# Both heads of a pair in one product: the scans of a hybrid mixer with block-diagonal queries and states

## The chip, the cores and the metric

The kernel runs on one core of a Trainium2 chip. TensorE (PE in the profile; its weight loads PEld) multiplies, VectorE (DVE), ScalarE (ACT) and GpSimd (POOL) do the rest of the arithmetic, and SyncE (SP) issues the DMAs. The metric is the device time of one launch in microseconds; the comparison is between the kernel before and the kernel with the change.

## The reference

A trunk of two layers over 1024 tokens of width 1024. The first layer's mixer splits one projection between four mLSTM heads and four retention heads, each with keys and queries of 64 and values of 128; the second is a Mamba-2 mixer; each is followed by an MLP. Only the first mixer changes. Both of its groups run over chunks of 128 tokens with a carried state. For retention (mLSTM has gates in place of the constant decay, and a normaliser that is carried as one more column of the state):

```python
s = jnp.einsum('bcthk,bcshk->bctsh', q, k) * decay
intra = jnp.einsum('bctsh,bcshv->bcthv', s, v)
d_r = jnp.einsum('lh,bclhk,bclhv->bchkv', w_k, k, v)
def step(r, dr):
    return chunk_decay[:, None, None] * r + dr, r
_, r_prev = lax.scan(step, jnp.zeros((bsz, nh, dk, dv), F32), jnp.moveaxis(d_r, 1, 0))
inter = w_q[None, None, :, :, None] * jnp.einsum('bcthk,bchkv->bcthv', q, r_prev)
return (intra + inter).reshape(bsz, seq, nh, dv)
```

## The kernel before

The residual stream lies in SBUF for the whole kernel. Large products are made of three products of high and low parts (`proj_in` at L136, `proj_nat` at L152, `proj_out` at L180). A tile framework derives the waits and, when the program is built, an order for each engine's queue: instructions that are ready are taken by their place in the program, so later work moves into gaps of earlier work, and the queues then run in that fixed order.

`hybrid` goes through the eight heads in four pairs, in the order 2, 3 (retention), 0, 1 (mLSTM). For a pair it projects values into `va` (tokens on partitions), then q and k into `qT` and `kT`, with head j of the pair on partitions 64j to 64j+63, tokens along the free dimension. Then comes the scan over eight chunks, then two gate projections (`hgate`), the head norm, and the output projection. Each scan's chunk does the following, all in fp32:

- L490 transposes k of both heads into PSUM (`tr`), L497 scales it by token into `kw`.
- L508, per head: scores, `kT` by `qT` on that head's 64 partitions, into the head's own PSUM tile `bank[j]`.
- L515 and L521 (mLSTM) or L523 (retention), per head: the scores under the decay mask, into `pt`.
- L528: queries scaled for the carried state, `qs`.
- L536 and L540, per head: `pt` by values, then `qs` by the carried state on 64 partitions, added up in the same PSUM tile; L543 copies the sum to `num`.
- L548, per head: `kw` by values into 64 of the 128 partitions of `dc`; L553 or L555 makes the new state from the old one and `dc`, both heads in one instruction, since the state of head j lies on partitions 64j to 64j+63.

The scan of a pair takes four PSUM tiles a chunk from a pool of five (`sc`). `headnorm` (L687 to L709) takes statistics of `num` on VectorE and two powers a half on GpSimd (L702, L706 for their kinds of pair). The weights' split into high and low parts is on ScalarE (L93) and VectorE (L94). The small tile `hnwr` (L402 to L406) holds the head norms' weights until they are transposed, early in the kernel. In the second mixer, L829, L838, L843 and L858 are the transposes and products of its scan, L832 a scaling of a transposed tile.

## Time and profile before

| | us |
|---|---|
| time, median of 3 runs | 2815.06 (2813.73 to 2817.12) |
| time of the profiled execution | 2813.8 |
| its span, first to last instruction | 2812.0 |
| TensorE busy | 2735.5 (97%) |
| VectorE busy | 1696.3 (60%) |
| ScalarE busy | 933.9 (33%) |
| GpSimd busy | 500.3 (18%) |

Busy time of TensorE counts from the start of a matmul to a modelled end, and neighbours overlap; the distance between two starts is what a product costs the queue. The granted clock of TensorE is full but for a few short stretches (mean 0.993). A product of fp32 operands appears as two records, each of a weight load (PEld) and a matmul. In a row, 64*128 after the tile names means a stationary operand of 64 rows and 128 columns.

### The profile page before, as it was taken

How to read it: one execution, taken by the hardware profiler on the slowest of the kernel's cores; microseconds unless marked ns; L12 is line 12 of the kernel's file. 1: busy time of each engine (PE TensorE's matmuls, PEld its weight loads, DVE VectorE, ACT ScalarE, POOL GpSimd, SP SyncE). 2: the span in 40 equal slices, each digit the busy share in tenths (PEclk: the TensorE clock that was granted, in tenths of full speed). 3: DMA queues.
4: the chain of work that ended last, by engine and by line, in shares of the span. 5: the costliest groups of instructions: out<-in, count | busy, mean ns of one | idle time of the engine just before them, and what ended most of it. 6: DMA issues, size and time to landing. Idle time of an engine off the chain costs nothing.

```text
span 2812.0 us, 33165 instructions
## 1 busy us (share of the span) xinstructions
PE 2735.5 (97%) x13149; PEld 2206.2 (78%) x13149; DVE 1696.3 (60%) x2794; ACT 933.9 (33%) x1547; POOL 500.3 (18%) x454
## 2 busy tenths in 40 slices
PE   8999999999999999899999999999999999999997
PEld 7788787888888888687787777777778888888885
DVE  5544436645656445876667667666676566654457
ACT  5131223322222222443433434344344222222223
POOL 1000000322233222300000000000013222322223
PEclk9999999999999999899999999999999999999999
DMA  4021210211111111032212222122221111110111
GB/s 157 23 77 31 60 53 23 68 45 60 60 60 46 37 39 55 23 81 74 67 54 70 67 67 75 51 70 68 59 62 53 60 60 60 53 42 27 60 38 60
DMA packets 199050, 161.47 MB, mean 57 GB/s; under 512 B 8952, under 2 KB 177840, under 8 KB 198768
## 3 DMA queue, kind: packets, MB, share of 16 engines
q1 hardware_dynamic: 198896, 159.36, 19.3%
q8 instruction: 103, 1.69, 0.2%
q14 instruction: 51, 0.42, 0.0%
HBM read 154.68 MB, written 4.62 MB: 57 GB/s over the span
## 4 chain that ended last, share of the span: by engine, by line
PE 91%; DMA 4%; ACT 2%; DVE 2%; POOL 1%; issue 0%; SPq 0%; DVEq 0%; ACTq 0%; POOLq 0%
PE mmin L136 49%; PE mmout L260 21%; PE mmout L180 9%; DMA cb<-cs_d 4%; PE mmnat L152 3%; PE yp L838 1%; PE pt L223 1%; PE bank L536 1%; PE bank L540 1%; ACT cb L816 1%; POOL h L355 1%; DVE un L206 1%; PE dc L548 1%; PE mmin L162 1%; PE cbp L801 1%; PE bank L508 0%
## 5 line engine op out<-in xcount | busy, mean ns | idle before, releaser
L136 PE MATMUL mmin<-uh,whi 128*128 128x512 f32 (+1 forms) x2112 | 825.6, 391 | 0.3 <-ACT uh L225 0.3
L136 PE MATMUL mmin<-ul,whi 128*128 128x512 f32 (+1 forms) x2112 | 825.9, 391 | 0.0
L136 PE MATMUL mmin<-uh,wlo 128*128 128x512 f32 (+1 forms) x2112 | 822.3, 389 | 0.0
L136 PEld LDWEIGHTS mmin<-uh,whi 128*128 128x128 f32 x2112 | 397.3, 188 | 90.8 <-issue 1.2
L136 PEld LDWEIGHTS mmin<-uh,wlo 128*128 128x128 f32 x2112 | 397.6, 188 | 88.0 <-issue 0.2
L136 PEld LDWEIGHTS mmin<-ul,whi 128*128 128x128 f32 x2112 | 397.6, 188 | 86.9
L94 DVE TENSOR_TENSOR wlo<-raw,whi 128x1024 fp32r<-128x1024 f32 x240 | 309.8, 1294 | 222.8 <-ACT whi L93 220.0
L93 ACT CAST whi<-raw 128x1024 fp32r<-128x1024 f32 (+1 forms) x243 | 251.1, 1038 | 461.0 <-PE mmin L136 220.4
L260 PE MATMUL mmout<-whi,hl 128*128 128x512 f32 x896 | 354.0, 395 | 0.7 <-DVE hl L94 0.7
L260 PE MATMUL mmout<-wlo,hh 128*128 128x512 f32 x896 | 353.9, 395 | 0.0
L260 PE MATMUL mmout<-whi,hh 128*128 128x512 f32 x896 | 353.9, 395 | 0.0
L180 PE MATMUL mmout<-whi,hid 128*128 128x512 f32 x768 | 245.5, 398 | 0.8 <-ACT hid L600 0.8
L311 DVE TENSOR_TENSOR q<-q 128x512 f32<-128x512 f32 x128 | 95.2, 744 | 221.9 <-ACT q L310 221.9
L283 DVE TENSOR_TENSOR h<-h,mmout 128x512 f32<-128x512 f32 x320 | 208.9, 679 | 33.2 <-PE mmout L260 33.0
L260 PEld LDWEIGHTS mmout<-whi,hl 128*128 128x128 f32 x896 | 168.7, 188 | 40.8 <-DVE hl L94 1.1
L260 PEld LDWEIGHTS mmout<-wlo,hh 128*128 128x128 f32 x896 | 168.7, 188 | 39.7
L260 PEld LDWEIGHTS mmout<-whi,hh 128*128 128x128 f32 x896 | 168.7, 188 | 39.8
L774 DVE SCALAR_TENSOR_TENSOR sact<-xr,cw,sact 128x512 f32<-128x512 f32 x192 | 144.2, 751 | 56.0 <-ACT sact L770 51.6
L180 PEld LDWEIGHTS mmout<-whi,hid 128*128 128x128 f32 x768 | 143.5, 188 | 36.1 <-ACT hid L600 2.5
L310 ACT ACTIVATE q<-mmin 128x512 f32<-128x512 f32 x128 | 76.3, 596 | 269.6 <-PE mmin L136 269.6
L180 PE MATMUL mmout<-wlo,hid 128*128 128x512 f32 x384 | 150.2, 395 | 0.0
L93 ACT CAST hh<-q 128x1024 fp32r<-128x1024 f32 x80 | 84.1, 1051 | 198.8 <-PE mmout L260 110.0
(374 smaller groups left out, 3178.8 us busy)
## 6 DMA issues: line engine op xcount, KB each, us to landing
raw<-in_mlp_w_dram SPq DMA_DIRECT2D x64, 512.0 KB
raw<-in_mlp_w_dram SPq DMA_DIRECT2D x32, 1024.0 KB
raw<-in_ssd_w_in_dram SPq DMA_DIRECT2D x48, 512.0 KB
cb<-cs_d SPq DMA_DIRECT2D x64, 256.0 KB
raw<-in_hyb_w_in_dram SPq DMA_DIRECT2D x24, 512.0 KB
raw<-in_ssd_w_out_dram SPq DMA_DIRECT2D x16, 512.0 KB
eh<-ecs_d SPq DMA_DIRECT2D x64, 128.0 KB
h<-in_x_dram SPq DMA_DIRECT2D x8, 512.0 KB
```

What stands on the lines that cost most here:

```text
L93: self.nc.scalar.copy(hi, raw)
L94: self.nc.vector.tensor_sub(lo, raw, hi.bitcast(F32))
L136: self.nc.tensor.matmul(ps[:, o : o + n], a[:, k], u[:, k, s], start=(k == 0 and i == 0), stop=(k == 7 and i == 2),)
L152: self.nc.tensor.matmul(ps, u[:, k, s], a, start=(k == 0 and i == 0), stop=(k == 7 and i == 2))
L162: self.nc.tensor.matmul(ps, w[:, k], u[:, k, s], start=(k == 0 and i == 0), stop=(k == 7 and i == 1))
L180: self.nc.tensor.matmul(ps, a[:, s], w[:, n], start=(kk == 0 and i == 0), stop=(kk == 1 and i == 2))
L206: nc.vector.scalar_tensor_tensor(un[j], self.h[:, c, n], r, wb[j], op0=ALU.mult, op1=ALU.mult)
L260: nc.tensor.matmul(banks[t], a[x][:, kk, s], w[y][:, kk], start=(not more and kk == 0 and i == 0), stop=(not more and kk == 1 and i == 2), ...
L283: nc.vector.tensor_add(y, y, x[t])
L310: nc.scalar.activation(x, ps, AF.Relu)
L311: nc.vector.tensor_mul(x, x, x)
L774: nc.vector.scalar_tensor_tensor(t, xr[:, k : k + HALF], cw[:, k, jt : jt + 1], t, op0=ALU.mult, op1=ALU.add)
```

## The change

The scan of a pair makes one product where it made one for each head. The queries of the two heads are copied by GpSimd into a tile `qbd` of 128 partitions and two blocks of 128 columns, head 0's queries in the upper half of the first block and head 1's in the lower half of the second; the other halves were set to zero once, ahead of the pairs. One product of `kT` with it gives the scores of both heads side by side in `sco`. The state is kept in the same form, two blocks of columns with zeros in the halves that belong to the other head, so one product of `qs` with it starts the sum `av` for both heads, and the two products of `pt` and values are added to it. One product of `kw` with the values of both heads gives `dc` with four blocks, of which the two that are wanted go into the state by two instructions of 64 partitions each. The masks of both heads are applied in one instruction, and one copy takes both heads' sums to `num`. `qbd` and the state have two buffers each, which alternate from chunk to chunk; `hnwr` moves into a rotating buffer of the mixer to make room.

```diff
--- before.py
+++ after.py
@@ -399,7 +399,7 @@
             wq = C[:, 640:896].rearrange("p (x t) -> p x t", x=2)
             wk_ret = C[:, 896:900]
             cdec = C[:, 900:902]
-            nwr = one.tile([8, P], F32, name="hnwr")
+            nwr = self.z_tile("hnwr", F32, (8, P))
             nc.sync.dma_start(nwr[0:4], m_norm_w.rearrange("(h p) -> h p", p=P))
             nc.sync.dma_start(nwr[4:8], r_norm_w.rearrange("(h p) -> h p", p=P))
             tp = self.sc.tile([P, HALF], F32, name="tp", tag="sc")
@@ -410,6 +410,16 @@
             rp = two.tile([P, 2, T], F32, name="rope", tag="wide", bufs=1)
             nc.sync.dma_start(rp, rope)
             nat = None
+
+
+            qbd = [one.tile([P, 2, P], F32, name=f"qbd{x}") for x in range(2)]
+            states = [one.tile([P, 2, P + 1], F32, name=f"state{x}") for x in range(2)]
+            heads = [slice(j * 64, (j + 1) * 64) for j in range(2)]
+            for j, r in enumerate(heads):
+                for x in qbd:
+                    nc.gpsimd.memset(x[r, 1 - j], 0.0)
+                for x in states:
+                    nc.gpsimd.memset(x[r, 1 - j], 0.0)
             for pair in (2, 3, 0, 1):
                 ml = pair < 2
                 p2 = pair % 2
@@ -499,30 +509,30 @@
                             tr.rearrange("p (h d) -> p h d", h=2),
                             wkc.broadcast_to([P, 2, 64]),
                         )
-
-                        bank = [
-                            self.sc.tile([P, HALF], F32, name="bank", tag="sc") for _ in range(2)
-                        ]
-                        for j in range(2):
-                            r = slice(j * 64, (j + 1) * 64)
-                            nc.tensor.matmul(
-                                bank[j][:, 0:P], kT[half][r, s], qT[half][r, s], start=True, stop=True
-                            )
+                        qb = qbd[c % 2]
+                        for j, r in enumerate(heads):
+                            nc.gpsimd.tensor_copy(qb[r, j], qT[half][r, s])
+                        sco = self.sc.tile([P, 2, 2 * P], F32, name="sco", tag="sc")[:, 0]
+                        nc.tensor.matmul(
+                            sco,
+                            kT[half][:, s],
+                            qb.rearrange("p h t -> p (h t)"),
+                            start=True,
+                            stop=True,
+                        )
+                        sco = sco.rearrange("p (h t) -> p h t", h=2)
                         pt = two.tile([P, 2, P], F32, name="pt", tag="pt")
-                        for j in range(2):
-                            if ml:
-                                hd = pair * 2 + j
+                        if ml:
+                            for j in range(2):
                                 nc.scalar.activation(
                                     pt[:, j],
                                     nm[:, j, c * P : (c + 1) * P],
                                     AF.Exp,
-                                    bias=nat[:, 0, hd, c : c + 1],
+                                    bias=nat[:, 0, pair * 2 + j, c : c + 1],
                                 )
-                                nc.vector.tensor_mul(pt[:, j], pt[:, j], bank[j][:, 0:P])
-                            else:
-                                nc.vector.tensor_mul(
-                                    pt[:, j], decay[:, p2 * 2 + j], bank[j][:, 0:P]
-                                )
+                            nc.vector.tensor_mul(pt, pt, sco)
+                        else:
+                            nc.vector.tensor_mul(pt, decay[:, p2 * 2 : p2 * 2 + 2], sco)
                         if c > 0:
                             qs = two.tile([P, P], F32, name="qs", tag="qs")
                             nc.vector.tensor_mul(
@@ -530,36 +540,36 @@
                                 qT[half][:, s],
                                 scb[:, s] if ml else wq[:, p2],
                             )
+                        av = self.sc.tile([P, HALF], F32, name="av", tag="sc")[:, 0 : 2 * W]
+                        av = av.rearrange("p (h d) -> p h d", h=2)
+                        if c > 0:
+                            nc.tensor.matmul(av, qs, state[:, :, 0:W], start=True, stop=False)
                         for j in range(2):
-                            r = slice(j * 64, (j + 1) * 64)
-                            av = bank[j][:, P : P + W]
                             nc.tensor.matmul(
-                                av, pt[:, j], va[:, j, 0:W], start=True, stop=(c == 0)
-                            )
-                            if c > 0:
-                                nc.tensor.matmul(
-                                    av, qs[r], state[r, 0:W], start=False, stop=True
-                                )
-                            nc.scalar.copy(num[:, cc, j, 0:W], av)
+                                av[:, j], pt[:, j], va[:, j, 0:W], start=(c == 0), stop=(c == 0 or j == 1)
+                            )
+                        nc.scalar.copy(num[:, cc, :, 0:W], av)
                         if c < NCH - 1:
-                            dc = self.sc.tile([P, HALF], F32, name="dc", tag="sc")
-                            for j in range(2):
-                                r = slice(j * 64, (j + 1) * 64)
-                                nc.tensor.matmul(
-                                    dc[r, 0:W], kw[:, j], va[:, j, 0:W], start=True, stop=True
-                                )
-                            new = two.tile([P, P + 1], F32, name="state", tag="state")
-                            if c == 0:
-                                nc.vector.tensor_copy(new[:, 0:W], dc[:, 0:W])
-                            else:
-                                nc.vector.scalar_tensor_tensor(
-                                    new[:, 0:W],
-                                    state[:, 0:W],
-                                    scb[:, cc * P + P - 1 : cc * P + P] if ml else cdec[:, p2 : p2 + 1],
-                                    dc[:, 0:W],
-                                    op0=ALU.mult,
-                                    op1=ALU.add,
-                                )
+                            dc = self.sc.tile([P, HALF], F32, name="dc", tag="sc")[:, 0 : 2 * W]
+                            dc = dc.rearrange("p (h d) -> p h d", h=2)
+                            nc.tensor.matmul(
+                                dc, kw.rearrange("p h d -> p (h d)"), va[:, :, 0:W], start=True, stop=True
+                            )
+                            new = states[c % 2]
+                            for j, r in enumerate(heads):
+                                if c == 0:
+                                    nc.vector.tensor_copy(new[r, j, 0:W], dc[r, j])
+                                else:
+                                    nc.vector.scalar_tensor_tensor(
+                                        new[r, j, 0:W],
+                                        state[r, j, 0:W],
+                                        scb[r, cc * P + P - 1 : cc * P + P]
+                                        if ml
+                                        else cdec[r, p2 : p2 + 1],
+                                        dc[r, j],
+                                        op0=ALU.mult,
+                                        op1=ALU.add,
+                                    )
                             state = new
                 gs = []
                 for j in range(2):
```

## Rows read from the trace of the kernel before

**Rows 1.** The page, part 1: engine, busy us, share of the span, instructions.

```profile
PE 2735.5 (97%) x13149; PEld 2206.2 (78%) x13149; DVE 1696.3 (60%) x2794; ACT 933.9 (33%) x1547; POOL 500.3 (18%) x454
```

**Rows 2.** Busy time in windows, sum over the four scans (lengths in rows 3).

```profile
sum 105.78, PE 105.78 PEld 69.31 DVE 66.42 ACT 34.69 POOL 7.29; mean PE 26.45 PEld 17.33 DVE 16.60 ACT 8.67 POOL 1.82
```

**Rows 3.** The same windows, projection matmuls of L136 alone: us, PE, weight loads.

```profile
66.66:96.30 29.64, 7.72 (x22) 3.32 (x21) 1.00 0.06 18
191.43:221.24 29.81, 8.69 (x28) 4.46 (x28) 1.00 0.23 71
307.14:330.30 23.16, 3.32 (x11) 1.46 (x10) 1.00 0.29 90
420.44:443.61 23.17, 3.33 (x10) 1.46 (x9) 1.00 0.09 24
```

**Rows 4.** Timeline of TensorE in the other mixer: start, us, engine, line, operation.

```profile
1255.05 0.59 PE L858 MATMUL ds__9484<-xw,bn 128*128 128x256 f32 x2
1255.48 0.49 PE L829 MATMUL tr<-ident,sact 128*128 128x128 f32 x3
...
1256.04 0.40 PE L136 MATMUL mmin<-ul,whi 128*128 128x512 f32 x1
...
1256.74 0.40 PE L136 MATMUL mmin<-ul,whi 128*128 128x512 f32 x1
```

**Rows 5.** Timeline of TensorE, one chunk of pair 2.

```profile
82.06 0.33 PE L490 MATMUL tr<-ident,hact 128*128 128x128 f32 x1
82.32 0.49 PE L508 MATMUL bank<-hact,hact 64*128 64x128 f32 x4
82.74 0.50 PE L136 MATMUL mmin<-uh,whi 128*128 128x512 f32 x1
...
84.60 0.49 PE L536 MATMUL bank<-va,pt 128*128 128x128 f32 x2
85.01 0.48 PE L540 MATMUL bank<-state,qs 64*128 64x128 f32 x2
85.43 0.43 PE L548 MATMUL dc<-va,kw 128*64 128x128 f32 x2
85.79 0.33 PE L490 MATMUL tr<-ident,hact 128*128 128x128 f32 x1
```

**Rows 6.** Timeline of TensorE, transposes a chunk apart in pair 0.

```profile
313.84 0.33 PE L490 MATMUL tr<-ident,hact 128*128 128x128 f32 x1
...
316.23 0.33 PE L490 MATMUL tr<-ident,hact 128*128 128x128 f32 x1
```

**Rows 7.** Timeline of TensorE, chunk 0 of pair 2.

```profile
68.07 0.71 PE L536 MATMUL bank<-va,pt 128*128 128x128 f32 x4
68.72 0.43 PE L548 MATMUL dc<-va,kw 128*64 128x128 f32 x2
```

**Rows 8.** Groups by line and form, 60 to 480 us.

```profile
L94 DVE TENSOR_TENSOR wlo<-raw,whi 128x1024 fp32r<-128x1024 f32 x27 | 32.7, 1221 | 54.7 <-ACT whi L93 54.6
...
L523 DVE TENSOR_TENSOR pt<-hyc,bank 128x128 f32<-128x128 f32 x32 | 8.0, 284 | 2.1 <-PE bank L508 0.4
...
L706 POOL TENSOR_TENSOR hsc<-hsc,mhalf 128x8 f32<-128x8 f32 x4 | 7.4, 1850 | 188.4 <-DVE hsc L705 188.4
...
L555 DVE SCALAR_TENSOR_TENSOR state<-state,scb,dc 128x129 f32<-128x129 f32 x12 | 4.2, 349 | 6.9 <-PE dc L548 6.9
```

**Rows 9.** Instructions on tile tr: count, min/median/max ns, first and last start.

```profile
L832 DVE TENSOR_TENSOR xd<-tr,dnat x64: 408/418/425, 1253.2 to 2084.8; 128x256 f32<-128x256 f32 x64
```

**Rows 10.** Timeline of GpSimd at the start.

```profile
1.01 0.29 POOL masks.py:199 TENSOR_SCALAR_AFFINE_SELECT ident<-ident 128x128 f32<-128x128 f32 x1
```

**Rows 11.** Groups by line and form, 500 to 900 us.

```profile
L94 DVE TENSOR_TENSOR wlo<-raw,whi 128x1024 fp32r<-128x1024 f32 x42 | 56.0, 1333 | 36.0 <-ACT whi L93 36.0
...
L290 POOL TENSOR_TENSOR s<-q 128x512 f32<-128x512 f32 x10 | 12.9, 1291 | 59.5 <-DVE q L311 59.5
```

**Rows 12.** Windows, the other mixer: us, PE, PEld, DVE, ACT, POOL busy.

```profile
1500.00:2083.00 583.00, 559.87 (x2803) 445.30 (x2803) 395.53 (x723) 237.90 (x480) 38.60 (x81) 0.99 0.25 67
```

## The prediction

> **What bounds the kernel now.** I read the page first: TensorE's instructions cover 97% of the span [rows 1]. A share that high says nothing by itself, because the end of a matmul is modelled; what counts is how far apart the starts lie, so the timeline of the stage that changes was read next. The change lies in four scans of eight chunks, one scan for each pair of heads. From the first transpose of k to the last product of states they take 29.64, 29.81, 23.16 and 23.17 us, together 105.78 us of the profiled execution's 2812.0 us [rows 2, 3]. TensorE is covered for all of it, VectorE for 66.42 us, ScalarE for 34.69 us, GpSimd for 7.29 us [rows 2]. So each scan is bound by TensorE's own queue; between its small products stand projection matmuls of the gates (L136), which are wanted anyway and merely move.
>
> Their number is 21, 28, 10 and 9 weight loads [rows 3]; two of these begin at the end of a stretch, so 66 belong to it. In an undisturbed run three of them start 0.70 us after one another, 0.233 us each [rows 4], so they are 15.4 us of the 105.8, and the scans' own products hold TensorE for the other **90.4 us**.
>
> Why so long? A product of fp32 operands is recorded as two passes, each a weight load and a matmul. In pairs 2 and 3 one chunk takes 3.73 us with two projections in it, so 3.26 us of its own [rows 5]; in pairs 0 and 1 it takes 2.39 us with none [rows 6]. In the first, one head's product of pt and values takes 0.41 us to the next start, one head's product of states and queries 0.42, one head's dc 0.36, the transpose 0.26, and the scores of both heads together 0.42 [rows 5]. The reader is to see that the shapes alternate: 128*128, then 64*128, then 128*64. Where two pt products stand side by side in chunk 0, the four passes take 0.65 us [rows 7], so the second costs some 0.23, not 0.41. In the other mixer a product of 128*128 with 256 columns, standing between other 128*128 products, takes 0.43 us from start to start, its weight load hidden; three transposes and one projection behind it take 0.56, which leaves 0.11 for a transpose [rows 4]. So about 0.2 us of each small product is not arithmetic: it is paid where the shape of the stationary tile changes.
>
> **The change, part by part.** *TensorE.* Scores of both heads become one 128*128 product with 256 columns, the two dc products another, the two products of states and queries a third; the two pt products stay, side by side. Every product of the scan is now 128*128. By [rows 4, 7] a chunk costs 3 x 0.43 + 2 x 0.23 + 0.11 = 1.86 us; chunk 0 (no states yet) and chunk 7 (no dc) 1.43. A pair: 6 x 1.86 + 2 x 1.43 = 14.0 us; four pairs 56.1. The saving on TensorE is 90.4 - 56.1 = **34.3 us**, if its queue stays fed. Check by steady chunks alone: 16 x (3.26 - 1.86) + 16 x (2.39 - 1.86) = 30.9, and the end chunks are dearer than that.
>
> A rule speaks against the merge. The Trainium skill, "TensorE: Matmul & The Clock Gate", Part 3, says that products on different row groups run at the same time, so zeros in a block-diagonal operand would buy nothing. The trace agrees for the scores: four passes in 0.42 us [rows 5], as much as the merged 0.43; by that rule alone the merge of the scores would save 0. It does not hold for the states here, whose two products stand apart.
>
> *VectorE.* The two masks of pt (0.284 us each) become one of 256 columns; the nearest row, a product of PSUM and SBUF of that size, takes 0.418 [rows 8, 9]: -0.15 us in 32 chunks, -4.8. The update of the state becomes two of 64 partitions; an instruction on fewer partitions is no shorter, as I take it, so 0.349 us more [rows 8] in 28 chunks, +9.8. VectorE gets 5 us more: 66.4 + 5 = 71.4 us. TensorE's own demand is 56.1 + 15.4 = 71.5. The two engines come out level, so the slack that VectorE had is gone: this is the cover that TensorE's old slowness gave, and where the next stall will be.
>
> *GpSimd.* Two copies of 64x128 a chunk build the block-diagonal queries. No such copy is in the trace. The nearest rows are 0.29 us for a read and write of 128x128 [rows 10] and 1.29 us for a sum of 128x512 [rows 11]; the first is nearest in columns, and fewer partitions need not make it shorter, so it is the lower end too, and I take it: 0.6 us a chunk, 2.6 at the upper end, against a chunk of 2.2 us with its projections. With two buffers a copy for chunk c+2 waits only for the scores of chunk c, and q is ready long before; hidden. Behind it in GpSimd's queue stands the headnorm's power of 1.85 us [rows 8], one or two in a scan: with two buffers of lead that costs a fraction of a microsecond.
>
> The Trainium skill, "SBUF — State Buffer", section "Who interferes with whom", says that a VectorE instruction with two SBUF inputs and a GpSimd instruction that reads SBUF exclude each other. The trace bears it out in part: the same split of weights takes 1.221 us while GpSimd is nearly idle and 1.333 us beside its sums [rows 8, 11]. By that rule each of some 8 such VectorE instructions of a scan could wait for one copy, 8 x 0.29 x 4 = 9 us on VectorE; I count it with the second case below and not in the sum.
>
> *The rest, one answer each.* ScalarE copies both heads' numerators at once: less work on an engine with two thirds of the stretch free [rows 2]. PSUM: four tiles a chunk before and after, the scores' bank now free after the mask. The eight memsets of zeros run on an idle GpSimd at the start. The norm weights' small tile moves to a rotating buffer, so its two DMAs wait in the sync queue until a slot is free, and what is queued behind them there (rotation tables, weights) waits too; first use of the result is a gate, long after; at most a microsecond, taken as 0.
>
> *Stalls.* The nearest scan with all tiles 128 wide and projections between is the other mixer's: TensorE is covered for 559.87 of 583.00 us, 4% open, with VectorE at 68% [rows 12]. On 71.5 us that is 2.9 from below. From above: if VectorE could be kept at no more than 84% (halfway between that 68% and full), 71.4 us would need 85, 13.5 us of stalls. I take 7, nearer to the row that is a measured one. So 34.3 - 7 = 27.3 us. The profiled execution's own time is 2813.8 us (span 2812.0); 2813.8 - 27.3 = 2786.5. The median of the runs is 1.3 us higher, 2815.06: **2788 us**. All that follows the scans (headnorm, output projection, MLP) is again bound by TensorE, so the gain should reach the end whole.
>
> **The rivals.**
> *VectorE becomes the pace.* The scans wait for it: stalls of 13.5 to 23 us instead of 7, by the demand above and the port rule. Gain 11 to 21, some 2799 us. For it: 71.4 us of demand against 71.5. Against: statistics for the headnorm and splits of later weights run there too, and need not run within the scan.
> *The price lies in fp32, not in the change of shape.* Then the 0.19 us between 0.42 and 0.23 is paid by each merged product as well: 0.62 each, transpose 0.26, two pt 0.65, 2.77 a chunk (2.15 in chunks 0 and 7), 83.7 us in all; the saving of 6.7 goes in the 7 of stalls: 2815 us, no change. Against: [rows 4] show 256 columns at 0.43 with nothing exposed. That the change doesn't do what it says is this case.
> *GpSimd becomes the pace, and it is slower.* Every chunk's scores wait for two copies in series. The old stretches are 105.78 us for 32 chunks, 3.3 us each, so the point is a copy of 1.65 us: above it the kernel is slower than before. At 1.9 us it is 32 x 3.8 = 122 us, 16 more, 2830 us. For it: an operation on 128x8 takes 1.85 us on this engine [rows 8]. Against: that is a power; a plain pass of 128x128 takes 0.29 [rows 10].
>
> **How the numbers follow.** Forecast (2779 to 2794) 0.60; VectorE paces 0.21; price in fp32 0.07; GpSimd paces 0.07; a gain above 34 us 0.05. About 0.2% (5.6 us) is what a measurement of this kernel can tell from no change. Faster: 0.60 + 0.21 + 0.05 = 0.86; same 0.07; slower 0.07. For 8 in 10 the range runs from 2779 (no stalls) to 2804 (the far end of the VectorE case).
>
> **What will show it.** Right, if in the timeline of a scan the merged products start 0.43 us apart, the pt products 0.23, the transpose 0.11, every form is 128*128, and the four scans with their projections take 75 to 85 us; the projections left after a scan grow or shrink by what the order moves, and no stage after it changes. Wrong, if merged products start 0.6 apart (the price in fp32), if weight loads wait for masks or states on VectorE by over 3 us a scan (VectorE's pace), or for the queries' copies (GpSimd's); or if a later stage gives the gain back by waiting for weights.

## The result, and the profile after

The kernel with the change takes **2785.19 us** (median of 4 runs, 2782.45 to 2786.53), the kernel before 2815.26 beside it: a ratio of 0.9892, 95% interval 0.9874 to 0.9909. The profiled execution took 2785.3 us, its span 2783.5, so the span is 28.5 us shorter. 27.4 us of that stand at one place: the first product of the first MLP (L260) starts 541.0 us into the span before and 513.6 after. What follows lasts 2271.0 and 2269.9 us.

The page, part 1 (engine, busy us, share of the span, instructions):

```profile
PE 2706.2 (97%) x12973; PEld 2195.3 (79%) x12973; DVE 1702.9 (61%) x2790; ACT 928.1 (33%) x1515; POOL 526.6 (19%) x526
```

TensorE's share is 97% as in [rows 1]: it tells nothing of the change. The windows of the four scans do (us; then PE, PEld, DVE, ACT and POOL busy with their instructions; granted clock, DMA share, GB/s), here pairs 2 and 0 and the sum of all four:

```profile
66.35:86.65 20.30, 18.86 (x102) 14.92 (x100) 17.50 (x64) 5.94 (x12) 6.52 (x13) 1.00 0.09 27
...
291.57:308.81 17.24, 17.24 (x95) 13.40 (x93) 16.13 (x68) 7.66 (x21) 5.04 (x15) 1.00 0.26 81
...
sum 75.01, PE 72.13 PEld 56.69 DVE 67.54 ACT 26.80 POOL 23.12; mean PE 18.03 PEld 14.17 DVE 16.89 ACT 6.70 POOL 5.78
```

105.78 us [rows 2] have become 75.01. VectorE's work is almost the same, 66.42 and 67.54 us, but it now fills 90% of the stretch instead of 63%, and TensorE is open for 2.88 us where it was open for none (shorter waits lie under the modelled ends of its matmuls). The same windows with the projections alone:

```profile
66.35:86.65 20.30, 6.94 (x18) 2.99 (x17) 1.00 0.09 27
182.92:203.15 20.23, 6.75 (x16) 3.06 (x17) 1.00 0.33 105
291.57:308.81 17.24, 4.03 (x11) 1.74 (x10) 1.00 0.26 81
398.85:416.09 17.24, 4.03 (x11) 1.74 (x10) 1.00 0.12 32
```

17, 17, 10 and 10 weight loads, of which one in each window begins at its end, so 50 belong to the scans, 16 fewer than in [rows 3]. They are 11.65 us at 0.233; the scans' own products hold TensorE for 75.01 - 11.65 = 63.4 us, before for 90.4. That is the figure by which kernels are compared below ("own"), because projections that move out of a scan have to be paid behind it.

TensorE's timeline of one chunk of pair 2 (start, us, engine, line, operation):

```profile
81.09 0.27 PE L500 MATMUL tr<-ident,hact 128*128 128x128 f32 x1
81.19 0.60 PE L516 MATMUL sco<-qbd,hact 128*128 128x256 f32 x2
81.44 0.58 PE L136 MATMUL mmin<-ul,whi 128*128 128x512 f32 x1
81.86 0.59 PE L546 MATMUL av<-state,qs 128*128 128x256 f32 x2
82.29 0.59 PE L555 MATMUL dc<-va,kw 128*128 128x256 f32 x2
82.72 0.61 PE L548 MATMUL av<-va,pt 128*128 128x128 f32 x4
83.17 0.27 PE L500 MATMUL tr<-ident,hact 128*128 128x128 f32 x1
```

The reader is to see that every shape is 128*128. Scores and projection together take 0.67, states 0.43, dc 0.43, both pt products 0.45, the transpose 0.10: 2.08 us from transpose to transpose, 1.85 without the projection, against 3.26 in [rows 5].

Not every chunk runs so. Two waits of 1.44 us, one in pair 2 and one in pair 3, are the longest in the scans. All engines' timeline around the first (in brackets the idle time ahead of the instruction and what ended it):

```profile
82.48 1.65 POOL L716 TENSOR_TENSOR hsc<-hsc,mhalf 128x8 f32<-128x8 f32 x1 [2.02 <-DVE hsc L715]
...
84.16 0.60 DVE L719 TENSOR_SCALAR num<-num,bmv,hsc 128x128 f32<-128x128 f32 x2 [1.57 <-POOL hsc L716]
84.68 0.72 DVE L563 SCALAR_TENSOR_TENSOR state<-state,hyc,dc 64x128 f32<-64x128 f32 x2
...
85.55 0.67 PE L546 MATMUL av<-state,qs 128*128 128x256 f32 x2 [1.44 <-DVE state L563]
```

Read from the bottom: TensorE waits for the state; dc, its input, was started at 82.29 (fence above), but in VectorE's queue the scaling of the head norm (L719) stands ahead of it, and that waits 1.57 us for a power on GpSimd (L716). VectorE is idle meanwhile. The wait is one of order, not of load.

### The profile page after: what moved, and what is told of

It reads as the page before. It is cut to its first block, busy times and chain, and to the rows that moved or that the text cites. A ratio compares the mean times of both kernels' runs of the same rounds, so it can differ in the third digit from the quotient of the medians.

```text
span 2783.5 us, 32858 instructions
## 1 busy us (share of the span) xinstructions
PE 2706.2 (97%) x12973; PEld 2195.3 (79%) x12973; DVE 1702.9 (61%) x2790; ACT 928.1 (33%) x1515; POOL 526.6 (19%) x526
## 4 chain that ended last, share of the span: by engine, by line
PE 90%; DMA 4%; ACT 2%; DVE 2%; POOL 1%; issue 0%; SPq 0%; DVEq 0%; ACTq 0%; POOLq 0%
PE mmin L136 49%; PE mmout L260 22%; PE mmout L180 9%; DMA cb<-cs_d 4%; PE mmnat L152 3%; PE yp L848 1%; PE pt L223 1%; ACT cb L826 1%; POOL h L355 1%; DVE un L206 1%; PE mmin L162 1%; PE cbp L811 1%; PE av L546 0%; PE tr L839 0%; PE sp L924 0%; PE av L548 0%
## 5 line engine op out<-in xcount | busy, mean ns | idle before, releaser
L136 PE MATMUL mmin<-uh,whi 128*128 128x512 f32 (+1 forms) x2112 | 826.7, 392 | 0.3 <-ACT uh L225 0.3
L136 PE MATMUL mmin<-ul,whi 128*128 128x512 f32 (+1 forms) x2112 | 825.6, 391 | 0.0
L136 PE MATMUL mmin<-uh,wlo 128*128 128x512 f32 (+1 forms) x2112 | 823.5, 390 | 0.0
L136 PEld LDWEIGHTS mmin<-uh,whi 128*128 128x128 f32 x2112 | 397.3, 188 | 89.8 <-issue 1.2
L136 PEld LDWEIGHTS mmin<-uh,wlo 128*128 128x128 f32 x2112 | 397.4, 188 | 88.5 <-issue 0.2
L136 PEld LDWEIGHTS mmin<-ul,whi 128*128 128x128 f32 x2112 | 397.3, 188 | 86.8
L260 PE MATMUL mmout<-whi,hl 128*128 128x512 f32 x896 | 353.7, 395 | 0.7 <-DVE hl L94 0.7
L260 PE MATMUL mmout<-wlo,hh 128*128 128x512 f32 x896 | 353.7, 395 | 0.0
L260 PE MATMUL mmout<-whi,hh 128*128 128x512 f32 x896 | 353.6, 395 | 0.0
L260 PEld LDWEIGHTS mmout<-whi,hl 128*128 128x128 f32 x896 | 168.6, 188 | 41.0 <-DVE hl L94 1.1
L260 PEld LDWEIGHTS mmout<-wlo,hh 128*128 128x128 f32 x896 | 168.6, 188 | 39.9
L260 PEld LDWEIGHTS mmout<-whi,hh 128*128 128x128 f32 x896 | 168.6, 188 | 39.9
```

The costliest lines, as they stand in the source:

```text
L136: self.nc.tensor.matmul(ps[:, o : o + n], a[:, k], u[:, k, s], start=(k == 0 and i == 0), stop=(k == 7 and i == 2),)
L260: nc.tensor.matmul(banks[t], a[x][:, kk, s], w[y][:, kk], start=(not more and kk == 0 and i == 0), stop=(not more and kk == 1 and i == 2), ...
```

## The experiments

They ran on chips on which the kernel before took 2820.6, 2820.6 and 2818.8 us, so times stand as ratios to it, and the scans as the sum of their four windows. "Shape changes" counts along TensorE's timeline of the four scans, up to the product that follows each, how often a product's stationary shape differs from that of the one ahead of it. "Arithmetic" is the sum of the scans' own products at the prices without a change: 0.11 a transpose, 0.22 a product of states or dc, 0.23 of pt, 0.43 a merged one, and 0.22 for two heads' products that stand side by side on different halves of the array (their rows are read below). How often they stand so is counted in each order: dc in 10 of 28 chunks of the kernel before, in all 28 with the scores alone and in 2 with the states alone; scores on 64 rows in all of 32 chunks but 5 (before), 2 (states alone), 4 (dc alone) and 2 (scores back on 64 rows).

| kernel | ratio | 95% interval | scans, us | L136 in them | own, us | shape changes | arithmetic, us |
|---|---|---|---|---|---|---|---|
| before | 1 | | 105.78 | 66 | 90.4 | 234 | 48.8 |
| after | 0.9892 | 0.9874 to 0.9909 | 75.01 | 50 | 63.4 | 0 | 56.1 |
| scores only | 0.9942 | 0.9927 to 0.9957 | 109.05 | 142 | 76.0 | 144 | 50.5 |
| states only | 0.9953 | 0.9935 to 0.9971 | 106.48 | 115 | 79.7 | 175 | 49.6 |
| dc only | 0.9966 | 0.9954 to 0.9978 | 97.78 | 58 | 84.3 | 180 | 50.5 |
| all shapes full, nothing merged | 0.9915 | 0.9898 to 0.9931 | 75.22 | 44 | 65.0 | 0 | 57.0 |
| scores back on 64 rows | 0.9918 | 0.9904 to 0.9932 | 81.26 | 58 | 67.7 | 68 | 49.8 |
| norm behind | 0.9890 | 0.9872 to 0.9908 | 69.72 | 38 | 60.9 | 0 | 56.1 |
| scaling behind | 0.9882 | 0.9868 to 0.9896 | 71.57 | 48 | 60.4 | 0 | 56.1 |
| one update | 0.9908 | 0.9893 to 0.9923 | 78.91 | 60 | 64.9 | 0 | 56.4 |
| after, again | 0.9901 | 0.9882 to 0.9921 | 75.02 | 50 | 63.4 | 0 | 56.1 |
| scaling behind, again | 0.9898 | 0.9879 to 0.9917 | 71.56 | 48 | 60.4 | 0 | 56.1 |
| one update, scaling behind | 0.9893 | 0.9874 to 0.9912 | 72.39 | 58 | 58.9 | 0 | 56.4 |
| copies on ScalarE | 0.9896 | 0.9872 to 0.9921 | 75.23 | 50 | 63.6 | 0 | 56.1 |

Own time reaches the end of the mixer: the first product of L260, 541.0 us into the span before and 513.6 with the change, starts at 526.1, 529.9 and 535.6 with the scores, the states and dc alone, at 515.7 with all shapes full, and at 519.6 with the scores back on 64 rows.

### What TensorE pays for: one merge at a time

Each of the three single merges also moves `hnwr`, as the whole change does.

**The scores alone**, from the kernel before:

```diff
+                        for j, r in enumerate(heads):
+                            nc.gpsimd.tensor_copy(qb[r, j], qT[half][r, s])
+                        sco = bank[0][:, 0 : 2 * P]
+                        nc.tensor.matmul(
+                            sco, kT[half][:, s], qb.rearrange("p h t -> p (h t)"), start=True, stop=True
+                        )
...
-                            av = bank[j][:, P : P + W]
+                            av = bank[j][:, 2 * P : 2 * P + W]
```

> From the kernel before, only the scores of both heads become one 128x128 product (with GpSimd's copies and one PSUM tile for it); states and dc stay per head. Theory (a change of the stationary tile's shape costs TensorE some 0.19 us): in pairs 2 and 3 two of nine changes of shape go, -0.37 us a chunk, and the merged product costs 0.43 against 0.22 us of two heads side by side, so -0.15 us a chunk; in pairs 0 and 1 the scores had the shape of their neighbour, one change is added and 0.22 us, +0.4 us a chunk. Sum over 32 chunks +4 us: no gain, 2812 to 2822 us. Rival (the gain comes from the number of products, three merged out of eight a chunk): a third of the 34 us on TensorE, 2804 us.

It came out the other way: 0.9942, own 76.0 us, 14.4 less than before. The 2804.6 us of its time are what the rival had, so the time alone doesn't tell why. TensorE's timeline of a chunk of it shows why:

```profile
76.34 0.44 PE L555 MATMUL dc<-va,kw 128*64 128x128 f32 x4
76.71 0.33 PE L495 MATMUL tr<-ident,hact 128*128 128x128 f32 x1
76.88 0.60 PE L515 MATMUL bank<-qbd,hact 128*128 128x256 f32 x2
77.12 0.59 PE L136 MATMUL mmin<-uh,wlo 128*128 128x512 f32 x1
...
78.25 0.38 PE L543 MATMUL bank<-va,pt 128*128 128x128 f32 x2
78.56 0.48 PE L547 MATMUL bank<-state,qs 64*128 64x128 f32 x2
78.98 0.49 PE L543 MATMUL bank<-va,pt 128*128 128x128 f32 x2
79.40 0.48 PE L547 MATMUL bank<-state,qs 64*128 64x128 f32 x2
79.81 0.44 PE L555 MATMUL dc<-va,kw 128*64 128x128 f32 x4
```

The two heads' dc products, apart in 18 of 28 chunks before (0.36 for one head in [rows 5]), now stand side by side in every chunk: four passes in 0.37 us, no longer than one head's two. The order of the queue is made anew when the program is built, and my expectation had counted the changes in the order before. In this one 144 changes are left of 234, and the two dc products, on different columns of the array, run together.

**The states alone** (block-diagonal state, `av` of both heads started by one product, the state updated by two instructions of 64 partitions; scores and dc as before):

```diff
+                        if c > 0:
+                            nc.tensor.matmul(av, qs, state[:, :, 0:W], start=True, stop=False)
...
-                            if c > 0:
-                                nc.tensor.matmul(
-                                    av, qs[r], state[r, 0:W], start=False, stop=True
-                                )
```

> From the kernel before, only the states are block-diagonal: one 128x128 product of queries and states for both heads, added to by the two products of pt and values; scores and dc stay per head. Theory: three of nine changes of shape go in pairs 2 and 3 (-0.55 us a chunk), two of five in pairs 0 and 1 (-0.4 us), in the 28 chunks with a state -13 us, less some 2 us of waits: 2800 to 2808 us. Rival (number of products): 2804 us, so this run alone does not tell the two apart; the sum of the three parts does.

Own 79.7 us, 10.7 less.

**dc alone** (one product for both heads, into the packed state by two instructions of 64 partitions):

```diff
-                                nc.tensor.matmul(
-                                    dc[r, 0:W], kw[:, j], va[:, j, 0:W], start=True, stop=True
-                                )
+                            nc.tensor.matmul(
+                                dc, kw.rearrange("p h d -> p (h d)"), va[:, :, 0:W], start=True, stop=True
+                            )
```

> From the kernel before, only the two dc products become one 128x128 product, and the packed state is updated by two instructions of 64 partitions. Theory: three of nine changes of shape go in pairs 2 and 3 (-0.55 us a chunk); in pairs 0 and 1 one goes (-0.2 us), but the two products that ran side by side in 0.22 us now take 0.43, so nothing there. Sum -8 us: 2804 to 2812 us. Rival (number of products): 2804 us. The three parts alone together: by the theory some -17 us, far less than the whole change's 34 us on TensorE, because a change of shape goes only when both neighbours have one shape; by the rival the three parts add up to the whole, -28 us or more.

Own 84.3 us, 6.1 less. Own time less arithmetic, by the number of changes, is (90.4 - 48.8) / 234 = 0.178 us before, 25.5 / 144 = 0.177 with the scores alone, 30.1 / 175 = 0.172 with the states alone, 33.8 / 180 = 0.188 with dc alone. Four kernels with different orders agree on **some 0.18 us for a change of shape**.

The single gains add to 31.2 us, the whole gives 27.0. In the expectation of dc alone I had put some 17 us for the sum if changes of shape are paid, and the whole or more if the number of products is. The sum came out on the rival's side. The test was a bad one, because the 17 rested on the order of the queue before; the counts above, and the next kernel, have to decide. The sum is above the whole since the whole has 56.1 us of arithmetic where the others have 50 (merged scores cost 0.43 where the pair side by side costs 0.22), and 7.3 us of waits. In the three TensorE is open for 0.4 us at most; that its longer queue covers such waits there is likely, but not shown.

**All shapes full, nothing merged**, from the kernel with the change: each merged product is split into two of 128 columns, so there are as many products as before.

```diff
-                        nc.tensor.matmul(
-                            sco,
-                            kT[half][:, s],
-                            qb.rearrange("p h t -> p (h t)"),
-                            start=True,
-                            stop=True,
-                        )
+                        for j in range(2):
+                            nc.tensor.matmul(
+                                sco[:, j * P : (j + 1) * P], kT[half][:, s], qb[:, j], start=True, stop=True
+                            )
```

> From the changed kernel, each merged product is taken apart again into two of 128 columns, on the same full 128x128 operands with their zeros: as many products as before the change, but all of one shape. Theory (shape): a chunk costs TensorE 0.02 to 0.04 us more for each of three products, 2 to 4 us in all: 2785 to 2791 us, and the four scans 75 to 79 us. Rival (number of products): all but the gain from other sources is lost, 2805 to 2815 us.

Own 65.0 us, 1.6 over the kernel with the change, 25.4 under the kernel before. TensorE's timeline of a chunk:

```profile
79.72 0.27 PE L500 MATMUL tr<-ident,hact 128*128 128x128 f32 x1
79.83 0.61 PE L517 MATMUL sco<-qbd,hact 128*128 128x128 f32 x4
80.27 0.39 PE L544 MATMUL av<-state,qs 128*128 128x128 f32 x2
80.66 0.71 PE L553 MATMUL dc<-va,kw 128*128 128x128 f32 x4
81.21 0.39 PE L545 MATMUL av<-va,pt 128*128 128x128 f32 x2
81.43 0.39 PE L544 MATMUL av<-state,qs 128*128 128x128 f32 x2
81.66 0.39 PE L545 MATMUL av<-va,pt 128*128 128x128 f32 x2
81.88 0.27 PE L500 MATMUL tr<-ident,hact 128*128 128x128 f32 x1
```

One head's pt product takes 0.22 to the next start, one of states 0.23, where [rows 5] have 0.41 and 0.42. The gain is in the shapes, not in the number of products: there are as many as before the change, and 25.4 of the 27.0 us stay.

**Scores back on 64 rows**, from the kernel with the change: no block-diagonal queries and none of GpSimd's copies, two masks a chunk; all else merged.

```diff
-                            nc.gpsimd.tensor_copy(qb[r, j], qT[half][r, s])
...
+                            nc.tensor.matmul(
+                                bank[j][:, 0:P], kT[half][r, s], qT[half][r, s], start=True, stop=True
+                            )
```

> From the changed kernel, only the scores go back to one product a head on 64 partitions, with one mask a head; no block-diagonal queries, no copies on GpSimd. Theory (shape): two changes of shape a chunk come back (+0.37 us), the scores of two heads side by side cost 0.22 instead of 0.43 us, and VectorE gets 0.15 us a chunk more; 32 chunks: +5 us, 2787 to 2793 us. If GpSimd's copies or their hold on VectorE's port were what keeps the changed kernel above its TensorE sum (7 us of stalls), this run is faster than the changed kernel instead, 2778 to 2783 us.

Own 67.7 us, 4.4 more. Arithmetic falls by 6.3, but 68 changes come back, some 12 us; with them the merge of the scores, which saves nothing by its own price, pays after all. Without GpSimd's copies the waits don't go away. All engines' timeline in pair 0:

```profile
308.30 1.64 POOL L706 TENSOR_TENSOR hsc<-hsc,mhalf 128x8 f32<-128x8 f32 x1 [95.92 <-DVE bmv L692]
...
309.97 0.17 DVE L707 TENSOR_TENSOR hsc<-hsc,hr 128x8 f32<-128x8 f32 x1 [1.56 <-POOL hsc L706]
...
310.71 0.74 PE L540 MATMUL bank<-state,qs 128*128 128x258 f32 x2 [1.43 <-DVE pt L526]
```

It is the same wait for the same power, here ahead of a mask. Behind it the granted clock falls to the lower of its two levels (0.62 on average from 311 to 312 us, 0.50 from 312 to 314), and the scan ends at 311.96, so by this estimate some 0.4 of the 4.4 us are the clock's.

### What the waits are made of

**The scaling behind**: of the head norm, only the scaling of `num` is held on VectorE's queue behind the last mask and the last update of the state of its pair's scan.

```diff
-        for cc in range(CPH):
+        with self.tc.issue_after(after[0].ins), self.tc.issue_after(after[1].ins):
+            for cc in range(CPH):
...
```

> From the changed kernel, only the head norm's scaling of the numerators is held behind the scan's last state update and last mask; statistics stay where they were. Theory (the two long stalls are a matter of VectorE's queue order, not of its load): the two stalls of 1.43 us go, 2.9 us of the scans, pairs 2 and 3 take 18.8 us each instead of 20.3; pairs 0 and 1 are unchanged; 2782 to 2783 us. Rival (VectorE's load): the stall reappears elsewhere in the scan, no change.

Both waits of 1.44 us are gone. The same place in it, mixed timeline, and pair 2's window:

```profile
83.44 0.70 DVE L563 SCALAR_TENSOR_TENSOR state<-state,hyc,dc 64x128 f32<-64x128 f32 x2
...
84.28 0.67 PE L546 MATMUL av<-state,qs 128*128 128x256 f32 x2
...
84.73 1.11 DVE L720 TENSOR_SCALAR num<-num,bmv,hsc 128x128 f32<-128x128 f32 x4
```

```profile
66.83:85.39 18.56, 18.56 (x101) 14.70 (x99) 17.36 (x65) 5.92 (x12) 6.52 (x13) 1.00 0.11 29
...
sum 71.57, PE 71.56 PEld 56.25 DVE 67.26 ACT 26.76 POOL 23.08; mean PE 17.89 PEld 14.06 DVE 16.82 ACT 6.69 POOL 5.77
```

The update and the last mask now come first, the product of states waits for nothing, and the scaling follows. Pairs 2 and 3 lose 1.74 and 1.71 us (one projection of 0.23 each among it), pairs 0 and 1 nothing; VectorE is as busy as it was. Own time is 60.4 us, 3.0 less.

**The norm behind**: the same hold for every instruction of the head norm.

```diff
-                    self.headnorm(two, num, nat, pair, half, ml)
+                    with tc.issue_after(last.ins), tc.issue_after(mask.ins):
+                        self.headnorm(two, num, nat, pair, half, ml)
```

> From the changed kernel, all VectorE instructions of the head norm are held behind the scan's last state update and last mask in VectorE's queue. Theory: the stalls left in the scans (7.3 us of 75.0) are VectorE's: 1.43 us twice because a scaling of the head norm stands in VectorE's queue ahead of the state update and waits for GpSimd's power, and the rest because VectorE is 90% busy there. Without statistics in the scans both go: scans of 69 to 71 us, 2779 to 2782 us, if the gates' projections cover the head norm that is now later. Rival: the head norm's output is late for the output projection, the gain is lost there or the kernel is slower, 2785 to 2795 us.

VectorE's busy time in the scans falls to 59.01 of 69.72 us, 85%. Own time is 60.9, no better than with the scaling alone. The 69 to 71 us that I expected of the scans came, but 2.8 us of the difference are 12 projections fewer in them, and 4.8 us of waits are left (60.9 - 56.1) where the theory had none. The gain is not lost in the head norm, as the rival had it: L260 starts at 510.9, before the 513.6 of the kernel with the change; what follows took 2278.9 us here. Taking the statistics out of the scan is worth nothing more once the order is right.

**One update**: keys in block-diagonal form, dc by one product a head with exact zeros, so the state takes one instruction of 128 partitions and 256 columns instead of two of 64.

```diff
+                                dc[:, j], kwf[:, j * P : (j + 1) * P], va[:, j, 0:W], start=True, stop=True
...
+                                nc.vector.scalar_tensor_tensor(
+                                    new[:, :, 0:W],
...
+                                    dc,
```

> From the changed kernel, the keys for dc are block-diagonal too (zeros set once, VectorE writes the two blocks), dc is two products of 128 columns whose unwanted halves are exact zeros, and the state of both heads is updated by one VectorE instruction of 256 columns instead of two of 64 partitions. Theory (VectorE paces what is left): VectorE gives up some 0.25 us in 24 chunks, 6 us of its 67.5 us in the scans, TensorE pays 1 us more; the short stalls before the states' product shrink, 2 to 4 us of gain, 2781 to 2784 us. If the short stalls are the latency of one instruction after another and not VectorE's load, 0 to 1 us.

The update takes 0.48 us instead of 0.70, but own time is 64.9, 1.5 more: with another order there are four such waits instead of two, and TensorE is open for 5.78 us instead of 2.88. The gain of 2 to 4 us that I expected did not come. The wait in pair 2:

```profile
81.41 0.86 DVE L722 TENSOR_SCALAR num<-num,bmv,hsc 128x128 f32<-128x128 f32 x3 [1.54 <-POOL hsc L719]
82.19 0.48 DVE L568 SCALAR_TENSOR_TENSOR state<-state,hyc,dc 128x256 f32<-128x256 f32 x1
...
82.72 0.70 PE L550 MATMUL av<-state,qs 128*128 128x256 f32 x2 [1.28 <-DVE state L568]
```

**One update, scaling behind**: both edits, and in mLSTM pairs the multiplication ahead of the scaling is held too.

```diff
-            nc.vector.tensor_mul(sc, sc, r)
+            with self.tc.issue_after(after[0].ins), self.tc.issue_after(after[1].ins):
+                nc.vector.tensor_mul(sc, sc, r)
```

> One update of the state for both heads (block-diagonal keys) together with the head norm's instructions that wait for GpSimd's power held behind the scan. Theory: the four stalls of 1.3 to 1.5 us that the one update ran into were the power's, 5.7 us; without them its own time in the scans falls from 64.9 to some 59 us, 1 to 2 us below the 60.4 us of the version with the hold alone, since VectorE has less to do: 1 to 2 us faster than that version. Rival (the one update is itself slower, by its wider instruction on the path from dc to the next states' product): no faster than the hold alone, 60 to 62 us.

Own 58.9 us, the least of all, 2.5 over the arithmetic and 1.5 less than with the scaling behind alone; the ratio is 0.9893.

**Copies on ScalarE**, from the kernel with the change:

```diff
-                            nc.gpsimd.tensor_copy(qb[r, j], qT[half][r, s])
+                            nc.scalar.copy(qb[r, j], qT[half][r, s])
```

> From the changed kernel, the copies of the queries into their blocks are made by ScalarE in place of GpSimd. Theory (GpSimd's copies are hidden, its port costs VectorE nothing that counts): the scans' 75 us stay within 1.5 us, the time within 3 us of the changed kernel on the same chip. Rival (the shared port holds VectorE up): VectorE's instructions with two SBUF inputs become shorter and the scans lose 3 us or more.

Scans 75.23 us against 75.02, own 63.6 against 63.4: nothing changes.

**The kernel with the change and the one with the scaling behind, again**, on the chip of these last two:

> The changed kernel once more, unaltered, so that it stands beside the versions of this call on one chip: scans of 75 us in all, a ratio to the kernel before of 0.989.

> The version whose head norm's scaling is held behind the scan's last state update, once more beside the changed kernel on the same chip. Theory (queue order): scans of 71.6 us against 75.0, so 3 to 4 us less than the changed kernel; if what follows the scans differs by as much from run to run, the times alone don't tell them apart and the windows must.

The scans repeat to 0.01 us (75.02 and 71.56), and L260 starts at 514.9 and 509.2 (513.6 and 511.1 in the first comparison), so shorter scans do reach the end of the mixer. The totals don't repeat as well: the two kernels came out at 0.9892 and 0.9882 in the first comparison, 0.9901 and 0.9898 in the second. The 3 us by which the scans differ can be read in the windows and not in the time, and no kernel here beats the one with the change by more than a measurement can tell.

## Why the prediction was right, step by step

- **The forecast.** 2788 was predicted, 2785.2 came; 27.3 us were to be gained by the scans and own time fell by 27.05. The scans with their projections were to take 75 to 85 us and take 75.01, since fewer projections run in them than I left there (50, not 66). The lower end of the range, 2779 with no stalls, is 2780.8 by its own sum (2815.06 - 34.3).
- **TensorE's price.** A chunk was to cost 1.86 us and costs 1.85. Merged products stand 0.43 apart, pt products 0.45 for both, the transpose 0.10, every form is 128*128. The cause named there, the change of shape, is shown by the single merges (0.17 to 0.19 us a change) and by the kernel with all shapes full and nothing merged.
- **The stalls: the size was right, the make was not.** 75.01 - 11.65 - 56.1 = 7.3 us, against 7 taken. That the size was right is luck: 7 was picked between a measured 2.9 and a 13.5 worked out from VectorE's load, which was put too high, and load is not what made them. 2.9 us are the two waits for GpSimd's power by way of VectorE's queue, which the kernel with the scaling behind removes; I had put "a fraction of a microsecond" on that power, because I asked only what stands behind it in GpSimd's queue, and not what stands behind its reader in VectorE's. The other 4.4 us are spread over the chunks; the kernel with the scaling behind keeps them (60.4 - 56.1 = 4.3), with one update on top 2.5 are left. Weight loads of the products of states and of pt wait 0.17 to 0.39 us there, several of them for a mask; these waits were not taken apart further, no run removes them all, and their cause stays open.
- **VectorE's demand** was overestimated: 71.4 predicted, 67.54 measured. The masks and updates came as priced (0.409 to 0.412 a mask against 0.418; 0.342 to 0.345 an update of 64 partitions against 0.349, so half the partitions are not shorter). But the 66.42 us of before held other work of a longer stretch, and some of it moved out as the scans grew shorter: both instructions of L470 (2.42 us), scalings of the numerators (4.35 to 2.56 us) and statistics (13.17 to 12.47 at L687, now L697). The four splits of weights stayed. (The 9.8 us for the updates counted 28 chunks; in 4 of them it is a copy of 0.29 us.)
- **GpSimd's copies** take 0.292 us in the median, as taken. The copies on ScalarE change nothing: they were hidden.
- **VectorE becomes the pace** did not come true: 90% busy in the scans, yet taking 8 us of work off it gained nothing over the right order. What one update gained then, 1.5 us, is a shorter instruction between dc and the next product of states as much as it is less work; no run tells the two apart. The port rule that I had put into this case shows, but on the other engine (last section).
- **The price lies in fp32**: refuted by merged products 0.43 apart. **GpSimd becomes the pace**: refuted by copies of 0.29 us, and by the kernels without them on GpSimd (67.7 and 63.6 us own).
- **Expectations failed.** Of the scores alone the price a change was right and the count wrong, because I took the order of the queue as given; the sum of the three parts, 17 us expected and 31.2 measured, failed by the same step. Of the norm behind and of one update I expected gains from less load on VectorE; the first gained no more than the right order alone, the second nothing. The prediction itself was safe from the count, since in the whole no order of the scan's products has a change in it.

## What to carry to other kernels

Where small products of different stationary shapes alternate, count the changes of shape along the queue before counting columns: here each was worth 0.18 us, nearly as much as a small product itself (0.22), and zeros that made all shapes equal cost less than the changes they saved. After such a gain look not only at how busy the next engine is, but at what its queue holds ahead of the instruction that the bounding engine waits for: here one short operation that waited for a power of 1.65 us on a third engine cost TensorE 1.44 us. A single part of a change says little of the whole when the order is made anew at each build: count again in each.

## What the runs showed of the hardware

**A change of shape.** Some 0.18 us at TensorE each time the stationary tile's shape changes between 128*128, 64*128 and 128*64 (0.172, 0.177, 0.178, 0.188 in the scans of four kernels). The Trainium skill, "TensorEngine Tiling (Array Packing)", section "Key Properties", says that changing the mode of tiling drains the engine; the trace agrees in that each change costs time, and gives that price. Two fp32 products on different column halves ran together, four passes in 0.37 us with the change in it, as two did on different row halves [rows 5].

**Beside a split on VectorE, GpSimd's copy took longer, and the split did not.** GpSimd's copies on tile `qbd` (count, then min, median and max ns), and one of the four places, one in each scan, where a copy took 1.34 us, mixed timeline of pair 2:

```profile
L514 POOL COPY qbd<-hact x64: 282/292/1341, 54.2 to 410.7; 64x128 f32<-64x128 f32 x64
```

```profile
67.13 1.68 POOL L514 COPY qbd<-hact 64x128 f32<-64x128 f32 x2 [11.52 <-PE sco L516]
...
67.44 1.22 DVE L94 TENSOR_TENSOR wlo<-raw,whi 128x1024 fp32r<-128x1024 f32 x1
```

The second copy began at 67.47, just after VectorE's split of a weight, which reads two operands from SBUF, and ended at 68.81, just after it; the split took its usual 1.22 us [rows 8]. The pairs of copies that start at 183.75, 292.35 and 399.62 in the other three scans take 1.68 us too, with a split of 1.22 us begun just ahead of the second copy; these four are the only splits that a copy met. They cost the scans nothing that shows: with the copies on ScalarE the scans are as long (75.23 us). The Trainium skill, "SBUF — State Buffer", section "Who interferes with whom", says that a VectorE instruction with two SBUF inputs contends with a GpSimd instruction that reads SBUF, and that the order of issue decides who is blocked; the trace agrees in these four cases, in all of which the split came first.

**The same code takes different times later on.** From L260's first start to the end of the span the kernel with the change took 2269.9 us in one profiled execution and 2277.2 in another. Part of it lies where the second mixer begins. Two windows of each, the first execution above (columns as in the scans' windows, with the granted clock third from the end):

```profile
1140.00:1150.00 10.00, 4.46 (x20) 2.89 (x19) 7.68 (x11) 5.34 (x10) 5.90 (x6) 0.80 0.34 94
...
1170.00:1180.00 10.00, 9.95 (x65) 8.63 (x66) 6.27 (x13) 2.89 (x5) 0.10 (x1) 1.00 0.30 75
```

```profile
1140.00:1150.00 10.00, 5.67 (x22) 3.66 (x21) 7.85 (x11) 5.20 (x9) 7.19 (x6) 0.75 0.39 105
...
1170.00:1180.00 10.00, 9.32 (x41) 7.46 (x40) 4.59 (x11) 2.54 (x4) 0.10 (x1) 0.72 0.17 42
```

TensorE is open for about half of the first window, and in it the granted clock falls (a clock of 0.5 is 1.2 GHz); in the second execution a part of 1170 to 1180 is at the lower level again, in the first none. By the clock that is worth at most 2.8 us (10 x 0.28); the rest of the 7 was not traced. It is why differences under 4 us were read in windows.
